# One fused transformer block on one core: gate tiles, table lookups, load order and the last norm rearranged

## The chip, the cores and the metric

One core of a Trainium2 chip. The metric is device microseconds (us) of one execution; the number for a kernel is the median of its runs. Engines: PE is TensorE (matmul), DVE is VectorE, ACT is ScalarE, POOL is GpSimd, SP is SyncE, which here only issues loads.

## The reference, cut to what matters

512 tokens of width 2048 pass three sublayers, each followed by `layer_norm(ALPHA * x + h)`:

```
h = hybrid_mixer(x)            # chunked mLSTM branch + 16-head forgetting attention,
                               # each branch times sigmoid(gate), summed, times w_out
h = memory_cross_attention(x)  # 4 heads on 256 memory rows
h = peer_ffn(x):
    q  = x @ w_pq;  sc = q . sub_keys                # 8 heads, 2 x 128 keys
    top_s, top_i = top_k(sc, 16)                     # per half
    best_s, best_pos = top_k(top_s0[:,None] + top_s1[None,:], 16)
    idx = (top_i0 * 128 + top_i1)[best_pos];  g = softmax(best_s)
    out = sum_k gelu(x . expert_u[idx_k]) * g_k * expert_v[idx_k]   # 128 of 16384 experts per token
```

All inputs and the output are float32.

## The kernel before, in words

**Matmuls.** A float32 product is made of three fp32r matmuls. `load_raw` (line 153) loads 1 MB of weights into a raw tile by the SP queue; `shares` (170) casts it to the high part with ACT (line 183, two casts of 1024 columns) and subtracts for the low part with DVE (188) into a ring tile; `group_ws` (198) and `group_as` (237) multiply. Where the next raw tile lies is given by `raws["pools"]`, a rotation over pools. All loads of weights are on the SP queue, which takes them in order; which order that is, is set by a scheduler that simulates the program and may place instructions of one engine otherwise than they were written, unless `after` (96) ties two of them.

**Tokens.** Tokens 0 to 127 pass first (`ml0`, `fx0`), then 128 to 511 as one block of 384 (`ml1` from 564, `fx1` from 649). In `ml1` sigmoid gates were stored to `sgd` in DRAM; for each of four groups lines 639 to 641 load four of them back into `qk` tiles (six buffers), ahead of that group's weights on the SP queue; line 645 stores the products to `mg`, by ACT's queue, out of the same tiles. In `fx1` the 16 attention heads run inside the pool `fxa`; the first of the four gate groups (`wi[28]`) is woven into heads 12 to 14, but its sigmoids (655) write into the pool `fxg`, which opens only when `fxa` has been closed.

**Experts, first 256 tokens.** `job_u` and `job_v` gather one expert row per token from DRAM by POOL's indirect DMA (1034) and use it with one DVE instruction of 2048 columns (1054, 1070). `tick` hands out these jobs: each ring share adds `rate * cost * mult` to a credit, and a full credit starts a job. 256 jobs for tokens 128 to 255 are handed out from 2910 us on, at `rate = 256 / 980`, with `mult` 0.65 in the selection stage, 1.5 in the building of the gates, 0.86 after it.

**Experts, last 256 tokens.** No gather here: every expert is multiplied.

- Selection (loop at 1365): `Choice.run` makes scores and `select` (926) picks 16 of 128 per half. Its positions are turned into indices by comparing with `iota`, multiplying with the indices and summing (964 to 966), once per half, in f32. Between the eight selections `next_a` (1323) multiplies 1 MB of the expert table `uT` each: three times, seven times at the last. The raw tiles lie in `wp`, in `rw`, opened on the right side of SBUF, and in `gap`.
- Building (1382 to 1414): the gate of each expert and token is the product of two one-hot matrices. For four tokens at a time DVE compares `i1` and `i0` with `iota` (1400, 1403, 128x512 f32), ACT scales the second in place (1406), PE multiplies (1407), ACT copies out (1412). Two calls of `next_a` stand at its start, then one for every second quad.
- Main loop (`stage_o`, 1456): 8 groups of 16 expert blocks, each for two halves `dh` of the output width, 8 loads of `vD` per half. `stage_h` (1441) makes the gated activation of two blocks: it multiplies (1448) the stored or kept gelu (`gb`, `ga`) by the gate `G` and splits it (150, 151). All eight calls of a group fall into its first half, `dh == 0`, but for the first, which is made in the half before. `ask_g` and `ask_a` load what they need.
- End: `fin` (1513) and `fin_gathered` (1095) make the last norm on DVE with `fin_head` (1078, its square root on ACT) and `fin_tail` (1082), then store.

Of the kernel before, what the change touches and what calls it, by code (L numbers as in the profile page):

```python
# [21 lines left out]
P = 128  # L22
# [4 lines left out]
H = 256  # L27
# [22 lines left out]
def build(tc, I, out):  # L50
    nc = tc.nc
    NC_ = PKEYS
    with ExitStack() as ctx:
# [72 lines left out]
        ioti = cp.tile([P, P], I32, tag="ioti", name="ioti")  # L126
        nc.gpsimd.iota(ioti, pattern=[[1, P]], base=0, channel_multiplier=0)
        nc.vector.tensor_copy(iota, ioti)
# [13 lines left out]
        ei = [cp.tile([P, P], I32, tag=f"ei{t}", name=f"ei{t}") for t in range(2)]  # L142
# [10 lines left out]
        def load_raw(src, n=2048):  # L153
# [7 lines left out]
            nc.sync.dma_start(raw[:, :n], src)  # L161
# [125 lines left out]
        sgd = dp.tile([16, P, 384], F32, tag="sgd", name="sgd")  # L287
        mlk = dp.tile([ML_H, P, 256], F32, tag="mlk", name="mlk")
# [275 lines left out]
        def ml1(mp, X, hpool, hT):  # L564
# [73 lines left out]
            for g in range(4):  # L638
                sg = [mt("qk", 6, n) for _ in range(4)]
                for q in range(4):  # L640
                    nc.sync.dma_start(sg[q], sgd[g * 4 + q])

                def ev_b(s, b, sg=sg, g=g):
                    nc.vector.tensor_mul(sg[s], sg[s], b)
                    nc.scalar.dma_start(mg[g * 4 + s], sg[s])

                yield from group_ws(I["w_br_ml"][g], hT, 3, ev_b)

        def fx1(X, ypool, yT, galloc, G):
            n = 384  # L650
            sgf, gate_pool = [], []

            def ev_g(s, b):
                t = gate_pool[0].tile([P, n], F32, tag="sg", bufs=16, name=nm("sg"))
                nc.scalar.activation(t, b, AF.Sigmoid)  # L655
                sgf.append(t)

            g0 = group_ws(wi[28], X, 3, ev_g)
            with pool("fxa", side="right") as fp:
                def ft(tag, bufs, n=512):  # L660
                    return fp.tile([P, n], F32, tag=tag, bufs=bufs, name=nm(tag))

# [43 lines left out]
                for qd in range(4):  # L706
# [916 lines left out]
```

## Time and profile before

| | us |
|---|---|
| runs of the kernel | 4589.1, 4597.87, 4593.03; median 4593.03 |
| the profiled execution | 4602.5 |
| its span, first to last instruction | 4600.8 |
| PE, DVE, ACT, POOL busy | 4467.5, 3743.1, 2231.7, 871.0 |

The profile is of one execution. [...] DMA share is the mean busy share of the 16 DMA engines of the core. A wait is put down to what came last.

### The profile page before, as it was taken

Reading aid. Unit: us, or ns where it says so; the run is one execution under the profiler, and the core shown is the slowest. Engines: PE = TensorE matmul, PEld = TensorE weight load, DVE = VectorE, ACT = ScalarE, POOL = GpSimd, SP = SyncE. Lnnn points to the kernel's source line nnn. Section 1 sums busy time; section 2 is a strip of 40 time slices with the busy share of each in tenths; the row PEclk is TensorE's granted clock in tenths of the full one; section 3 lists DMA queues with packets and bytes.
Section 4 is the critical chain, followed back from the end, with each engine's and each line's share of the span. In section 5 each row is a group of like instructions: output and inputs, shape, how many; then the busy total and the mean of one; then the engine's idle time right before and its main releaser. Section 6 shows DMA issues by size and latency. Waiting matters only on the chain.

```text
span 4600.8 us, 65219 instructions
## 1 busy us (share of the span) xinstructions
PE 4467.5 (97%) x25702; PEld 3993.3 (87%) x25702; DVE 3743.1 (81%) x4326; ACT 2231.7 (49%) x3029; POOL 871.0 (19%) x631
## 2 busy tenths in 40 slices
PE   8999999999999999999999999898999999999997
PEld 7888888889888899999799777798998778999996
DVE  7877667657798877887778678799988988988888
ACT  6766766645344422333322585544774334434433
POOL 1000000000132222232122000011222323333332
PEclk9999999999999999999999999899999999999998
DMA  8898889766798889888789766786989999999997
GB/s 295 321 334 327 323 316 342 259 235 213 281 339 331 333 310 346 340 339 311 266 331 346 296 244 231 270 311 250 372 346 419 398 382 403 379 384 396 372 357 292
DMA packets 244019, 1488.70 MB, mean 324 GB/s; under 512 B 26588, under 2 KB 52252, under 8 KB 75392
## 3 DMA queue, kind: packets, MB, share of 16 engines
q1 hardware_dynamic: 150384, 888.47, 51.7%
q0 software_dynamic: 81664, 561.95, 31.2%
q10 hardware_dynamic: 11664, 34.12, 1.9%
q8 instruction: 201, 3.29, 0.3%
q14 instruction: 106, 0.87, 0.1%
HBM read 1425.15 MB, written 59.29 MB: 323 GB/s over the span
## 4 chain that ended last, share of the span: by engine, by line
PE 65%; DVE 6%; issue 5%; DMA 3%; POOL 1%; ACT 1%; DVEq 0%; SPq 0%; ACTq 0%; POOLq 0%
PE mm L209 22%; PE mm L259 6%; PE mm L251 6%; PE mm L252 6%; PE mm L1491 4%; PE mm L1490 4%; PE mm L1487 4%; PE pa L1343 4%; PE pa L1336 3%; PE pa L1339 3%; DVE ring L188 2%; POOL rows L1034 1%; DMA raw<-in_vD 1%; DVE rows L1054 1%; PE sm L700 1%
## 5 line engine op out<-in xcount | busy, mean ns | idle before, releaser
L183 ACT CAST ring<-raw 128x1024 fp32r<-128x1024 f32 x1568 | 1600.1, 1050 | 1528.4 <-PE mm L209 464.1
L188 DVE TENSOR_TENSOR ring<-raw,ring 128x2048 fp32r<-128x2048 f32 (+1 forms) x926 | 1813.2, 1961 | 542.5 <-ACT ring L183 267.8
L1034 POOL DMA_INDIRECT rows<-in_peer_u,ei x256 | 368.6, 1440 | 1634.9 <-DVE rows L1054 791.3
L209 PE MATMUL mm<-Ah,ring 128*128 128x384 f32 x2560 | 669.6, 341 | 2.4 <-ACT sg L655 2.4
L1034 POOL DMA_INDIRECT rows<-in_peer_v,ei x256 | 435.5, 1701 | 978.8 <-DVE x2l L1070 698.3
L1054 DVE SCALAR_TENSOR_TENSOR rows<-rows,x2l 128x2048 f32<-128x2048 f32 x256 | 583.9, 2284 | 34.2 <-DMA rows<-in_peer_u,ei 34.0
L1070 DVE SCALAR_TENSOR_TENSOR x2l<-rows,dots,x2l 128x2048 f32<-128x2048 f32 x256 | 600.7, 2347 | 11.9 <-DMA rows<-in_peer_v,ei 11.2
L1336 PE MATMUL pa<-Xh,ring 128*128 128x256 f32 x2048 | 495.0, 283 | 2.7 <-ACT ring L183 2.7
L1339 PE MATMUL pa<-Xl,ring 128*128 128x256 f32 x2048 | 492.0, 281 | 0.0
L209 PEld LDWEIGHTS mm<-Ah,ring 128*128 128x128 f32 x2560 | 462.9, 189 | 8.0 <-ACT sg L655 2.6
L209 PE MATMUL mm<-Al,ring 128*128 128x384 f32 x1280 | 429.1, 339 | 0.0
L1491 PE MATMUL mm<-ring,hpl 128*128 128x512 f32 x1024 | 394.8, 398 | 9.5 <-DVE hpl L151 9.5
L1490 PE MATMUL mm<-ring,hph 128*128 128x512 f32 x1024 | 393.4, 396 | 8.3 <-ACT ring L183 5.5
L1336 PEld LDWEIGHTS pa<-Xh,ring 128*128 128x128 f32 x2048 | 386.7, 189 | 6.1 <-ACT ring L183 3.5
L1339 PEld LDWEIGHTS pa<-Xl,ring 128*128 128x128 f32 x2048 | 387.5, 189 | 2.4
L251 PE MATMUL mm<-ring,Zh 128*128 128x512 f32 x832 | 328.1, 394 | 2.7 <-ACT ring L183 2.7
L252 PE MATMUL mm<-ring,Zl 128*128 128x512 f32 x832 | 328.7, 395 | 0.0
L251 PE MATMUL mm<-ring,Ah 128*128 128x512 f32 x768 | 307.5, 401 | 1.1 <-ACT ring L183 1.1
L252 PE MATMUL mm<-ring,Al 128*128 128x512 f32 x768 | 304.3, 396 | 0.0
L209 PE MATMUL mm<-Bh,ring 128*128 128x384 f32 x1024 | 263.2, 339 | 8.1 <-ACT ring L183 7.5
L1343 PE MATMUL pa<-Xh,ring 128*128 128x256 f32 x2048 | 265.8, 282 | 3.1 <-DVE ring L188 3.1
L1487 PE MATMUL mm<-ring,hph 128*128 128x512 f32 x1024 | 257.6, 392 | 2.4 <-DVE ring L188 2.2
(393 smaller groups left out, 7081.0 us busy)
## 6 DMA issues: line engine op xcount, KB each, us to landing
raw<-in_w_in SPq DMA_DIRECT2D x256, 1024.0 KB
raw<-in_uT SPq DMA_DIRECT2D x128, 1024.0 KB
raw<-in_vD SPq DMA_DIRECT2D x128, 1024.0 KB
raw<-in_w_out SPq DMA_DIRECT2D x48, 1024.0 KB
raw<-in_peer_wq SPq DMA_DIRECT2D x48, 1024.0 KB
raw<-in_w_xkv SPq DMA_DIRECT2D x32, 1024.0 KB
raw<-in_w_br_ml SPq DMA_DIRECT2D x32, 1024.0 KB
raw<-in_w_br_fx SPq DMA_DIRECT2D x32, 1024.0 KB
```

The source lines that it names most:

```text
L183: x = nc.scalar.copy(hi[:, c:c + 1024], src[:, c:c + 1024])
L188: s = nc.vector.tensor_sub(lo, src, hi.bitcast(F32))
L209: i = nc.tensor.matmul(o, w, x, start=start and s % per == 0, stop=stop and s % per == per - 1)
L251: nc.tensor.matmul(banks[t], xh[:, tt], wh[:, c], start=k == 0, stop=False)
L252: nc.tensor.matmul(banks[t], xl[:, tt], wh[:, c], start=False, stop=False)
L1034: i = nc.gpsimd.indirect_dma_start(out=rows, out_offset=None, in_=I[table], in_offset=bass.IndirectOffsetOnAxis(ap=ei[t][:, k:k + 1], axis=0))
L1054: i = nc.vector.scalar_tensor_tensor(rows, rows, 1.0, tok[t]["x2l"], op0=ALU.mult, op1=ALU.mult, accum_out=d[:, k % GB:k % GB + 1])
L1070: i = nc.vector.scalar_tensor_tensor(acc, rows, d[:, GB + k % GB:GB + k % GB + 1], acc, op0=ALU.mult, op1=ALU.add)
L1336: i = nc.tensor.matmul(bank, uh[:, sl], xh, start=k == 0, stop=False)
L1339: nc.tensor.matmul(bank, uh[:, sl], xl, start=False, stop=False)
L1490: nc.tensor.matmul(banks[t][g], a[:, tt], vh[:, gs_], start=c == c0, stop=False)
L1491: nc.tensor.matmul(banks[t][g], b[:, tt], vh[:, gs_], start=False, stop=False)
```

## The change

It consists of eight edits, A to H.

- A: the gate weights are loaded by the SP queue in place of ACT's.
- B: in `ml1` the four `sgd` loads of a group come after the group's second load of weights.
- C: in `fx1` the first two gate groups write into tiles of `fxa` and are stored to a new DRAM tensor `fgd`; the first is woven into all of heads 12 to 15, the second follows inside `fxa`. Groups 2 and 3 stay; `fgd` is loaded during group 3.
- D: `rw` is opened on the left side, after `gap`; the rotation and its start change; the next six loads of weights are tied to their written order; `keysT` is loaded after the third load of a group.
- E: `select` looks up both halves together, in bf16: ACT copies the indices to bf16, repeated 16 times, and DVE makes one compare, one multiply and one sum of 1024 columns.
- F: nine calls of `next_a` at the last selection, and none at the start of the building; `mult` 0.7 in place of 0.65 in the selection.
- G: in the building `i0` is compared in bf16, four tokens innermost; ACT scales out of that tile, reading every fourth element, into a new f32 tile.
- H: `stage_h` is called in both halves, every second load; in the last norm the subtraction of the mean and the product with the weight come before the square root's chain, and the last additions to `acc` are tied behind the first product of the gathered tokens' norm.

```diff
 A            gw = gp.tile([P, 16, 68], F32, tag="graw", name="gw")
-            nc.scalar.dma_start(gw, I["gate_w"])
+            nc.sync.dma_start(gw, I["gate_w"])
 B (ml1)
-                sg = [mt("qk", 6, n) for _ in range(4)]
-                for q in range(4):
-                    nc.sync.dma_start(sg[q], sgd[g * 4 + q])
+                sg = []
...
-                yield from group_ws(I["w_br_ml"][g], hT, 3, ev_b)
+                for i, _ in enumerate(group_ws(I["w_br_ml"][g], hT, 3, ev_b)):
+                    yield
+                    if i == 1:
+                        for q in range(4):
+                            sg.append(mt("qk", 6, n))
+                            nc.sync.dma_start(sg[q], sgd[g * 4 + q])
 C (fx1)
+                def gate_out(g):
+                    def ev(s, b):
+                        t = ft("c", 10, n)
+                        nc.scalar.activation(t, b, AF.Sigmoid)
+                        nc.scalar.dma_start(fgd[4 * g + s], t)
+                    return group_ws(wi[28 + g], X, 3, ev)
...
+                    g0 = gate_out(0)
                     for s in range(4):
-                        if qd == 3 and s < 3:
+                        if qd == 3:
                             yield next(g0)
                         fox_head(4 * qd + s, ...)
+                yield from gate_out(1)
             with pool("fxg", side="right") as gp:
-                gate_pool.append(gp)
-                yield from g0
-                for g in range(1, 4):
-                    yield from group_ws(wi[28 + g], X, 3, ev_g)
+                sgf = [gp.tile([P, n], F32, tag="sg", bufs=16, name=nm("sg")) for _ in range(16)]
+                for g in (2, 3):
+                    for i, _ in enumerate(group_ws(wi[28 + g], X, 3, ev_g)):
+                        yield
+                        if g == 3:
+                            for q in (2 * i, 2 * i + 1):
+                                nc.sync.dma_start(sgf[q], fgd[q])
 D
-        rw = rws.enter_context(pool("rw", side="right"))     # before xs.close(), bb.close()
+        rw = rws.enter_context(pool("rw"))                   # after gap is opened
-        raws["pools"], raws["one"] = [wp, rw, wp, rw, gap], gap
+        raws["pools"], raws["one"], raws["n"] = [wp, rw, wp, gap, rw], gap, -1
+        raws["order"] = (6, None)
...
-                        yield from group_ws(I["peer_wq"][g], X2, 2, ev_q)
+                        for i, _ in enumerate(group_ws(I["peer_wq"][g], X2, 2, ev_q)):
+                            yield
+                            if i == 2:
+                                after(ld.dma_start(ks, I["keysT"][:, 4 * g:4 * g + 4]), raws["last"])
 E (select)
-                ixf = w("ixf", [4, 16])
-                nc.vector.tensor_copy(ixf, ix)
+                ids = w("ids", [4, 16, 16], BF16, bufs=1)
+                nc.scalar.copy(ids, ix.unsqueeze(3).to_broadcast([P, 4, 16, 16]))
...
-                for q, n in ((0, "i0"), (1, "i1")):
-                    eq = w("eq", [2, 16, 16], bufs=1)
-                    nc.vector.tensor_tensor(eq, pf[:, q]..., it, op=ALU.is_equal)
-                    nc.vector.tensor_mul(eq, eq, ii[:, :, q]...)
-                    nc.vector.tensor_reduce(out=sel[n][t][:, sl]..., in_=eq, axis=AX.X, op=ALU.add)
+                eq = w("eq", [4, 16, 16], BF16, bufs=1)
+                nc.vector.tensor_tensor(eq, pf..., ranks..., op=ALU.is_equal)
+                nc.vector.tensor_mul(eq, eq, ids)
+                nc.vector.tensor_reduce(out=self.ids[t][:, :, sl]...,
+                                        in_=eq.rearrange("p (q h) r k -> p q h k r", q=2), axis=AX.X, op=ALU.add)
 F
-        state["mult"] = 0.65
+        state["mult"] = 0.7
-                    for i in range(7 if steps == 8 else 3):
+                    for i in range(9 if steps == 8 else 3):
...
-            if t == 0:
-                next_a()
-                next_a()
 G
-                    o0 = gp.tile(full, F32, tag="o0", bufs=3, name=nm("o0"))
-                    nc.vector.tensor_tensor(o0, selT["i0"][:, ta:ta + 4].unsqueeze(2).to_broadcast(full), it,
+                    o0 = gp.tile([P, P, 4], BF16, tag="o0", bufs=2, name=nm("o0"))
+                    nc.vector.tensor_tensor(o0, selT["i0"][:, ta:ta + 4].unsqueeze(1).to_broadcast([P, P, 4]), keys4,
                                             op=ALU.is_equal)
+                    og = gp.tile(full, F32, tag="og", bufs=2, name=nm("og"))
-                        hold = nc.scalar.activation(o0[:, u], o0[:, u], AF.Copy, scale=...)
+                        hold = nc.scalar.activation(og[:, u], o0[:, :, u], AF.Copy, scale=...)
 H (stage_o, fin, fin_gathered)
-                    nxt = c0 + 2 * jj + 2 if dh == 0 else c0 + J
-                    if nxt < c0 + J or (dh and jj == 6 and not last):
-                        stage_h(nxt)
+                    due = c0 + J + 2 * (jj // 2 + 1) if dh else c0 + (2 * jj + 4 if c0 == 0 else J // 2 + jj + 2)
+                    while nxt_h[0] < min(due, NC_, c0 + J + J // 2):
+                        stage_h(nxt_h[0])
+                        nxt_h[0] += 2
...
-                if dh and not last and jj < 2:
-                    ask_g(c0 + J + 4 * jj)
-                    ask_a(c0 + J + 2 + 2 * jj)
...
-                        nc.vector.tensor_add(o, o, banks[t][g])
+                        i = nc.vector.tensor_add(o, o, banks[t][g])
+                        if last and dh:
+                            after(i, first_norm)
...
+            nc.vector.bn_aggr(st[:, 24:26], st[:, 0:24])
+            for q in range(2):
+                fin_low(acc..., st, lw[0]...)       # (a - mean) * w
             fin_head(st)                            # 1 / sqrt(var + eps)
             for q in range(2):
-                fin_tail(acc[:, sl], st, lw[0][:, sl], lw[1][:, sl])
+                fin_high(acc..., st, lw[1]...)      # a * rstd + b
```

## Rows read from the trace of the kernel before

**Rows 1.** The page: the line of its first part (busy us, share, instructions), the granted clock in 40 slices, and from its fifth part the group of the casts (busy us, mean ns | idle before).
```profile
PE 4467.5 (97%) x25702; PEld 3993.3 (87%) x25702; DVE 3743.1 (81%) x4326; ACT 2231.7 (49%) x3029; POOL 871.0 (19%) x631
...
PEclk9999999999999999999999999899999999999998
...
L183 ACT CAST ring<-raw 128x1024 fp32r<-128x1024 f32 x1568 | 1600.1, 1050 | 1528.4 <-PE mm L209 464.1
```

**Rows 2.** Busy time by stretch. Columns: stretch, its length, busy us of PE, PEld, DVE, ACT and POOL with the count of instructions, granted clock, DMA share, GB/s.
```profile
1674.00:1690.00 16.00, 8.53 (x34) 8.21 (x33) 6.34 (x5) 2.78 (x3) 1.88 (x2) 0.68 0.66 265
2266.00:2300.00 34.00, 25.85 (x112) 18.87 (x111) 15.58 (x44) 11.70 (x27) 2.08 (x2) 0.86 0.39 140
2906.00:2932.00 26.00, 12.98 (x93) 12.27 (x91) 12.05 (x15) 10.48 (x16) 2.19 (x2) 0.74 0.67 252
3060.00:3180.00 120.00, 120.00 (x1013) 120.00 (x1012) 116.02 (x262) 50.98 (x57) 20.19 (x16) 1.00 0.81 306
3180.00:3210.00 30.00, 14.80 (x95) 13.75 (x94) 28.81 (x103) 11.52 (x26) 0.00 (x0) 0.66 0.30 117
3210.00:3420.00 210.00, 202.77 (x1695) 200.29 (x1695) 193.70 (x210) 157.16 (x409) 50.85 (x31) 1.00 0.90 350
...
3584.00:3607.00 23.00, 19.43 (x74) 15.05 (x73) 19.00 (x20) 7.13 (x8) 4.84 (x3) 0.87 0.94 371
3674.00:3710.00 36.00, 32.42 (x128) 25.66 (x127) 30.99 (x28) 14.39 (x17) 7.27 (x6) 0.91 0.95 376
3787.00:3810.00 23.00, 19.43 (x77) 15.09 (x76) 23.00 (x21) 8.39 (x10) 6.19 (x4) 0.93 0.90 342
3900.00:4500.00 600.00, 597.83 (x3851) 545.41 (x3850) 522.75 (x295) 244.44 (x270) 205.01 (x103) 1.00 0.95 379
...
4574.00:4601.00 27.00, 0.89 (x4) 0.37 (x2) 22.89 (x45) 0.61 (x3) 0.00 (x0) 0.56 0.29 117
```

**Rows 3.** The DMA queues: one issue of the whole program, with its size.
```profile
gw<-in_gate_w ACTq DMA_DIRECT2D x1, 544.0 KB
```

**Rows 4.** The chain of work that ended last, 1640 to 1695 us: start, us, what (xcount).
```profile
1643.62 9.33 PE mm L209 x54
...
1653.84 12.52 DMA mg<-qk
...
1667.03 15.45 DMA raw<-in_w_br_ml
...
1683.68 11.43 PE mm L209 x49
```

**Rows 5.** The same chain, end of the attention heads, 2220 to 2300 us.
```profile
2294.45 1.28 ACT L655
2295.75 0.50 ACT sg L655
2296.29 3.86 PE mm L209 x13
```

**Rows 6.** What the SP queue issued, 2850 to 2920 us: start, us, line, what (xcount, merged).
```profile
2888.48 24.42 SPq L161 DMA_DIRECT2D raw<-in_uT  x3
2913.00 0.41 SPq L161 DMA_DIRECT2D raw<-in_peer_wq  x1
```

**Rows 7.** The chain of work that ended last, 2905 to 2945 us.
```profile
2912.55 0.14 DVE ei L1020
...
2913.00 10.37 DMA raw<-in_peer_wq
...
2924.49 13.44 PE mm L209 x96
```

**Rows 8.** DVE's instructions in the selection stage, 2930 to 3200 us, by line and shape: busy us, mean ns of one | idle before.
```profile
L188 DVE TENSOR_TENSOR ring<-raw,ring 128x2048 fp32r<-128x2048 f32 x42 | 95.7, 2278 | 4.8 <-PE mm L209 3.8 <-issue 0.9
L1054 DVE SCALAR_TENSOR_TENSOR rows<-rows,x2l 128x2048 f32<-128x2048 f32 x29 | 66.1, 2281 | 5.0 <-DMA rows<-in_peer_u,ei 5.0
L964 DVE TENSOR_TENSOR eq<-pf,iota 128x512 f32<-128x512 f32 x16 | 11.0, 685 | 0.0
L965 DVE TENSOR_TENSOR eq<-eq,ixf 128x512 f32<-128x512 f32 x16 | 10.9, 684 | 0.0
L966 DVE TENSOR_REDUCE sel_i<-eq 128x32 f32<-128x512 f32 x16 | 10.9, 681 | 0.0
...
L980 DVE TENSOR_TENSOR sel_g<-sel_g,s 128x256 f32<-128x256 f32 x1 | 0.4, 420 | 0.0
```

**Rows 9.** The building of the gates, 3206 to 3425 us: two groups by line.
```profile
L1406 ACT ACTIVATE o<-o,gT 128x128 f32<-128x128 f32 x241 | 75.9, 402 | 13.2 <-DVE o L1403 12.6 <-DVE o L1400 0.4
...
L1403 DVE TENSOR_TENSOR o<-i0T,iota 128x512 f32<-128x512 f32 x60 | 40.8, 683 | 0.0
```

**Rows 10.** Who PE waited for, 3440 to 3860 us: us in total, times, longest.
```profile
PE mm L1491 <- DVE hpl L151: 9.5, 3, 3.2
```

**Rows 11.** DVE in order of time, 3580 to 3612 us: start, us, line, what [idle before].
```profile
3591.08 2.48 DVE L1502 SCALAR_TENSOR_TENSOR acc<-acc,mm 128x512 f32<-128x512 f32 x4 [4.00 <-PE mm L1487]
```

**Rows 12.** DVE in order of time, 4500 to 4601 us.
```profile
4573.76 2.48 DVE L1504 TENSOR_TENSOR acc<-acc,mm 128x512 f32<-128x512 f32 x4 [5.22 <-PE mm L1487]
4576.15 2.46 DVE L1099 BATCH_NORM_STATS2 fst<-x2l 128x6 f32<-128x512 f32 x4
...
4581.32 2.48 DVE L1083 SCALAR_TENSOR_TENSOR x2l<-x2l,fst,lw 128x1024 f32<-128x1024 f32 x2
```

More of the change, by code (lines that the diff above doesn't have):

```diff
@@ L125, in build @@
         iota = cp.tile([P, P], F32, tag="iota", name="iota")
-        ioti = cp.tile([P, P], I32, tag="ioti", name="ioti")
-        nc.gpsimd.iota(ioti, pattern=[[1, P]], base=0, channel_multiplier=0)
-        nc.vector.tensor_copy(iota, ioti)
+        ei = [cp.tile([P, P], I32, tag=f"ei{t}", name=f"ei{t}") for t in range(2)]
+        nc.gpsimd.iota(ei[0], pattern=[[1, P]], base=0, channel_multiplier=0)
+        nc.vector.tensor_copy(iota, ei[0])
+        ranks = cp.tile([P, 16, 16], BF16, tag="ranks", name="ranks")
+        nc.vector.tensor_copy(ranks, iota[:, 0:16].unsqueeze(2).to_broadcast([P, 16, 16]))
         def const_in(name, shape):
@@ L160, in load_raw @@
                 raw = p.tile([P, 2048], F32, tag="raw", bufs=1 if p is raws.get("one") else 2, name=nm("raw"))
-            nc.sync.dma_start(raw[:, :n], src)
+            i = raws["last"] = nc.sync.dma_start(raw[:, :n], src)
+            if raws.get("order"):
+                if raws["order"][1] is not None:
+                    after(i, raws["order"][1])
+                raws["order"] = (raws["order"][0] - 1, i) if raws["order"][0] > 1 else None
             return raw
@@ L287, in build @@
         sgd = dp.tile([16, P, 384], F32, tag="sgd", name="sgd")
+        fgd = dp.tile([8, P, 384], F32, tag="fgd", name="fgd")
         mlk = dp.tile([ML_H, P, 256], F32, tag="mlk", name="mlk")
@@ L909, in __init__ @@
                 self.tp, self.nb, self.lean, self.gate = tp, nb, lean, None
-                self.sel = {n: [pl.tile([P, P], F32, tag=f"{n}{t}", name=nm(f"sel_{n}{t}")) for t in range(nb)]
-                            for n in ("i0", "i1")}
+                self.ids = [pl.tile([P, 2, P], F32, tag=f"i{t}", name=nm(f"sel_i{t}")) for t in range(nb)]
+                self.sel = {n: [i[:, q] for i in self.ids] for q, n in ((0, "i0"), (1, "i1"))}
                 self.gates = pl.tile([P, nb, P], F32, tag="g2", name=nm("sel_g"))
@@ L1380, in build @@
         gp = gs.enter_context(pool("gbuild", side="right"))
-        selT = {n: gp.tile([P, H], F32, tag=n + "T", name=n + "T") for n in ("i0", "i1", "g")}
+        selT = {n: gp.tile([P, H], d, tag=n + "T", name=n + "T") for n, d in (("i0", BF16), ("i1", F32), ("g", F32))}
+        keys4 = gp.tile([P, P, 4], BF16, tag="keys4", name="keys4")
+        nc.vector.tensor_copy(keys4, iota.unsqueeze(2).to_broadcast([P, P, 4]))
         for t in range(HB):
@@ L1401, in build @@
                                             op=ALU.is_equal)
[L1402 to L1403 removed]
+                    o0 = gp.tile([P, P, 4], BF16, tag="o0", bufs=2, name=nm("o0"))
+                    nc.vector.tensor_tensor(o0, selT["i0"][:, ta:ta + 4].unsqueeze(1).to_broadcast([P, P, 4]), keys4,
                                             op=ALU.is_equal)
+                    og = gp.tile(full, F32, tag="og", bufs=2, name=nm("og"))
                     for u in range(4):
[L1406 to L1407 removed]
+                        hold = nc.scalar.activation(og[:, u], o0[:, :, u], AF.Copy, scale=selT["g"][:, ta + u:ta + u + 1])
+                        nc.tensor.matmul(bank[:, u * P:(u + 1) * P], o1[:, u], og[:, u], start=True, stop=True)
                     if q % 2:
@@ L1514, in fin @@
             st = fst[t]
+            nc.vector.bn_aggr(st[:, 24:26], st[:, 0:24])
+            for q in range(2):
+                sl = slice(q * 1024, (q + 1) * 1024)
+                fin_low(acc[t][:, sl], st, lw[0][:, sl])
             fin_head(st)
```

53 lines of the change are left out of this document (24 added, 29 removed).

## The prediction, made before the change was run

> **What bounds the kernel now.** I read the page's busy line and its clock by slices first. PE has a matmul in flight for 4467.5 of 4600.8 us [rows 1], so the whole kernel is paced by PE, and what can be won without removing matmuls is the 133 us in which PE has none, plus the time in which the granted clock is below full after such a hole. The change removes no matmul, so only these holes count. The second view is the busy time by stretch: it shows that the holes are not spread evenly. From 3900 to 4500 us PE misses 2 us of 600; in six short stretches it misses 3 to 15 us each, and in these the granted clock is also down, 0.66 to 0.93 as a mean [rows 2]. The third view, the chain of waits, says for each hole what was late; the fourth, an engine in order of time, says why. The eight edits are priced hole by hole.
>
> **Edit B, the `sgd` loads.** PE is idle 7.5 of the 16 us at 1674, and the 49 matmuls behind the hole take 11.43 us where 54 took 9.33 before it, so they lose about 3 us to the lower clock [rows 2, 4]. The chain: the stores of the last products to `mg` (12.52 us) release the `qk` tiles, only then does SP issue the `sgd` loads, and behind them stands the next weight load, which lands 15.45 us later [rows 4]. With B two weight loads stand ahead of the wait, 96 matmuls at 0.173 us or 16.6 us of PE work, more than the 12.52 us store. Gain 10 us, ends 7 and 10.5. SP still waits there; what is late next is the third weight load.
>
> **Edit C, the gates behind the heads.** In 2266 to 2300 PE is idle 8.2 us, at a mean clock of 0.86, because the last heads have almost nothing beside them [rows 2]; then a table load (1.28 us) and a sigmoid stand before the first matmul, and 13 matmuls take 3.86 us, 1.6 more than at 0.173 [rows 5]. With C the rest of the first gate group and all of the second (96 x 2 matmuls, 33 us) need no new pool and can lie beside heads 14 and 15. New: 8 stores and 8 loads of 192 KB, 3.1 MB or some 9 us of DMA at the 350 GB/s of a busy stretch [rows 2], but spread over 70 us in which PE has no hole; the 8 loads stand on SP between weight loads into tiles long free, and two more table loads of 1.28 us fall on ACT, which works 11.7 of 34 us there. Those are covered; without the cover they would cost 2.6 us. Gain 9 us, ends 4 and 11.5.
>
> **Edit D, the start of the selection.** PE is idle 13.0 of the 26 us at 2906, and the 96 matmuls after it take 13.44 us where 96 at 0.118 take 11.4 [rows 2, 7]: 15 us in all. SP issued three `uT` loads from 2888 to 2913 ahead of the fourth `peer_wq` load, which PE needed first; it left SP at 2913.00, released by the indices of the block before (`ei`), and took 10.37 us to land [rows 6, 7]. With D the written order is kept, so this load goes first, and `rw` no longer lies where those indices keep tiles. I cannot see from the trace when the tiles beneath the new place come free; the norm of the block before runs until 2910, so the fifth load may wait that long, which PE would not feel, since four loads of 48 matmuls are 22.6 us. `keysT` now waits behind the third load on SP and can hold the fourth until the same tiles are free, which would leave some of the hole. Gain 11 us, ends 3 and 15.
>
> **Edit E, the lookup.** Per selection six instructions of 0.68 us go, 4.1 us of DVE [rows 8], and three of 1024 columns come. The trace has no two-operand DVE instruction in 16 bit. By elements, one costs 2278 / 2 = 1.14 us or a little more; by bytes, as 128x512 in f32, 0.68 us [rows 8]. [...] I take 0.9 for each of the other two, halfway, so E saves about 1.1 us of DVE per selection (0.6 to 1.5), 8 selections here, 9 us. ACT gains a copy of 1024 columns, 1.05 us [rows 1], and is half idle in this stage (50.98 of 120 us) [rows 2]. The trace shows a sum of 512 columns at 0.68 us over adjacent elements only [rows 8]. [...] No row here reads strided, so the bounds above stand.
>
> **Edits E and F, the end of the selection.** Here DVE is the limit: 116 of 120 us from 3060 to 3180 and 28.8 of 30 us after, while PE is idle 15.2 of the last 30 and then runs at a low clock, mean 0.66, some 3 us [rows 2]. F puts two calls of `next_a` (48 matmuls at 0.118, 5.7 us each, 11.4 us) from the building into this hole. They bring DVE two shares (4.6 us) and, with the ticks at the higher rate, about 1.5 + 2.4 jobs of 2.28 us, 9 us [rows 8], while E gives back 9. Half of the added jobs fall early in the stage, where DVE has slack, so DVE ends about 4 us later; the building loses 11.4 us of PE work. Gain 11.4 - 4, and 1 us of clock: 8 us, ends 3 and 14. Hidden behind this: the jobs moved here are missing from the building, and their number over the kernel is the same.
>
> **Edit G, the building.** PE is idle 7.2 of 210 us; DVE works 194, ACT 157, DMA is 0.90 busy [rows 2]. The 64 compares of 0.683 us [rows 9] become 0.42 each if bytes count (the 128x256 f32 row) or stay [rows 8]: 0 to 17 us of DVE. I take 0.55, 8 us, which lets DVE run ahead and closes part of PE's idle time: 2 us, ends -2 and 6, the lower one because the scaled tile now has two buffers where it had three. The trace shows f32 compares alone, at a time per element. [...]
>
> **Edit H, `stage_h` in both halves.** At the three stretches from 3584, 3674 and 3787 PE is idle 3.6 us each and runs at a mean clock of 0.87 to 0.93 [rows 2]; three waits for the low half `hpl` sum to 9.5 us [rows 10]. At the first, DVE waits 4.00 us for PE, makes four additions of `acc`, and only then the share and the activation that PE needs next [rows 11]. By count of matmuls: 74, 128 and 77 where 23, 36 and 23 us at 0.23 hold 100, 157 and 100, so 78 matmuls or 18 us are missing. With H four pairs of activations exist at each border. What is late next is the bank that the additions must free, about 0.7 us, and the weight share behind them. Gain 12 us, ends 5 and 16. From 3900 on 2 us are missing, and there is nothing to gain.
>
> **Edit H, the end.** The last matmul ends at 4574; then 27 us of DVE. Before it DVE is idle 5.22 us, although the gathered tokens' sums are complete: their statistics (2.46 us) and first product (2.48 us) come after the additions [rows 12]. The new tie puts these 4.9 us into the idle time. Gain 5 us, ends 2 and 6. **Edit A:** 544 KB off the first transfers are some 1.3 us at 416 GB/s and more [rows 2, 3]: 1 us, ends 0 and 1.5.
>
> **The sum.** 1 + 10 + 9 + 11 + 8 + 2 + 12 + 5 = 58 us; all lower ends give 22, all upper ends 81. The profiled execution took 4602.5 us, so 4544.5 by its own time; that execution lies 9.5 us above the median of the runs, 4593.03, and by the median the forecast is 4535 us.
>
> **Rivals.** (1) *The holes close, but DMA and DVE give a part back.* DMA is at 0.90 to 0.95 and DVE at 84 to 100% from 3060 us on [rows 2]; an earlier start there only meets the next wait. Then B, C and A hold (20 us), the end holds (5), and of D to H between a fifth and a third comes through, 10: 35 us, 4558. For it: those shares. Against: from 3900 to 4500 the same shares leave PE without a hole. (2) *A new wait on SP's queue takes the place of the one removed.* D and B only move loads that wait for tiles; if `keysT`, `sgd` or the fifth load holds a weight load as long as before, B and D give 0: 37 us, 4556. That both fail is unlikely, since the chain names what held each. (3) *Slower: ACT in the building.* Its scaling now reads every fourth element of a 16-bit tile. There are 256 of them at 0.402 us [rows 9], and ACT is busy 157 of 210 us [rows 2]. If a strided read cost 1 us, ACT would need 157 + 240 x 0.6 = 301 us, 91 more than the stretch lasts: with the other 56 us of gain that is 35 us slower, 4628. It decides from about 0.87 us each on (157 + 240 x 0.47 = 270, 60 over); below 0.62 it costs nothing. Nothing in the trace reads ACT's input so. (4) *The change does not do what it says,* as far as 16 bit goes: no compare is faster. Then E saves 5 in place of 9 and G gives 0: 6 us less, 4541, inside the forecast.
>
> **How the numbers follow.** A measurement of this kernel can tell about 0.2%, 9 us. Forecast with (4): 0.66; (1): 0.18; (2): 0.09; (3): 0.04; 0.03 for ends that cancel. The forecast's own range is 4512 to 4558. The range over the cases reaches from all upper ends, 81 us, less the spread of the runs, to the sum of all lower ends (4571), rounded: 4506 to 4570. Faster 0.92, same 0.04, slower 0.04.
>
> **What would show it right or wrong.** Right: in the profile after, no wait of `peer_wq` behind `uT`, the stretches that answer to 1674, 2266, 2906 and the three borders without a hole above 2 us and at a clock of 1.0, compares of 1024 columns between 0.61 and 1.2 us, and DVE busy in the 5 us before the last matmul. Wrong: ACT scalings above 0.5 us, PE idle at the end of the selection as long as before, or a new wait of SP for tiles in front of weights. A time above 4571 would mean that the holes moved instead of closing.

## The result and the profile after

The changed kernel took 4570.82 us (median of 4 runs, 4567.12 to 4573.15) beside 4595.45 of the kernel before on the same chip: ratio 0.9944, interval 0.9929 to 0.996. That is 25 us faster where 58 were forecast, just outside the range of 4506 to 4570. The profiled execution took 4572.07 us with a span of 4570.0, 30.8 under that of before. The lines of its page that answer to [rows 1]:

```profile
PE 4461.2 (98%) x25702; PEld 3983.3 (87%) x25702; DVE 3724.8 (82%) x4264; ACT 2252.1 (49%) x3051; POOL 900.4 (20%) x631
...
PEclk9999999999999999999999999999999999999999
...
L188 ACT CAST ring<-raw 128x1024 fp32r<-128x1024 f32 x1568 | 1597.1, 1050 | 1456.8 <-PE mm L214 454.1
```

The matmuls are the same 25702. The busy time by stretch, for the stretches of [rows 2] moved to where the same work now stands (columns as there), and one more, 3456 to 3578:

```profile
1665.00:1681.00 16.00, 14.77 (x85) 14.45 (x85) 10.65 (x10) 3.26 (x4) 4.30 (x3) 1.00 0.99 405
2244.00:2278.00 34.00, 34.00 (x199) 32.32 (x199) 29.18 (x38) 14.87 (x24) 5.82 (x6) 1.00 0.88 313
2881.00:2907.00 26.00, 20.86 (x145) 19.10 (x145) 15.74 (x28) 18.12 (x28) 3.68 (x2) 0.87 0.90 344
3155.00:3185.00 30.00, 13.31 (x86) 12.44 (x85) 28.94 (x88) 10.14 (x23) 0.94 (x1) 0.66 0.20 79
3185.00:3395.00 210.00, 203.94 (x1676) 200.67 (x1675) 178.57 (x204) 159.36 (x408) 36.99 (x31) 0.99 0.90 351
3456.00:3578.00 122.00, 112.98 (x528) 92.30 (x527) 103.03 (x91) 46.42 (x56) 32.13 (x19) 0.94 0.99 395
3567.00:3590.00 23.00, 22.69 (x97) 17.70 (x96) 22.33 (x20) 9.24 (x11) 7.03 (x4) 1.00 1.02 415
3656.00:3692.00 36.00, 35.65 (x153) 28.07 (x152) 33.22 (x30) 13.81 (x16) 9.97 (x6) 1.00 1.02 419
3763.00:3786.00 23.00, 22.38 (x95) 17.68 (x96) 23.00 (x21) 7.78 (x9) 7.28 (x4) 1.00 1.00 400
3875.00:4475.00 600.00, 598.46 (x3855) 546.02 (x3854) 523.98 (x295) 245.09 (x271) 215.03 (x103) 1.00 0.96 380
4548.00:4570.00 22.00, 0.88 (x4) 0.37 (x2) 18.30 (x37) 0.41 (x2) 0.00 (x0) 0.62 0.35 143
```

The holes of B, C and of the three borders are gone, and that at 2906 is mostly closed. The hole at the selection's end is as it was (PE 13.31 of 30 us, granted clock 0.66 of full). Worse than before is the stretch from 3456 to 3578: PE 113 of 122 us at a clock of 0.94, with DMA at 0.99. The same work in the kernel before:

```profile
3475.00:3592.00 117.00, 110.28 (x534) 91.23 (x533) 98.24 (x84) 46.38 (x54) 31.03 (x20) 0.97 1.01 412
```

So DMA was as busy there before, and PE missed 6.7 us in place of 9.0. In the changed kernel the chain of waits goes through transfers of 1 MB that take 21 us, 18 to 19 in that stretch before and 10.37 in [rows 7]. After:

```profile
3432.89 21.00 DMA rows<-in_peer_u,ei
...
3460.73 21.02 DMA raw<-in_vD
...
3519.97 21.25 DMA raw<-in_vD
```

Before:

```profile
3476.48 18.82 DMA raw<-in_vD
...
3533.44 18.00 DMA raw<-in_vD
```

To compare kernels I count the columns of the matmuls, which are the same in all, and read when PE has issued 3.2, 4.2, ... million of them (a "mark"). "Lost" is the time in a stretch without a matmul, plus the rest weighted by what the granted clock is below full. The three stretches are the selection's end with the building (6.49 to 6.88 million), the building's end with the first group of the main loop (to 7.27) and the three borders (to 7.82). From the traces, in us (one profiled execution of each kernel; "median" is that of all its runs):

```
kernel             at 3.2    4.2  6.02 M   lost: select  first  borders   at 7.82  9.2 M   span   median
before             1528.1 2013.8  2939.6          24.4   11.1     20.2     3860.8 4489.6  4600.8  4595.5
changed            1527.9 2004.8  2913.7          23.4   21.2      5.5     3835.6 4463.6  4570.0  4570.8
before_bc          1528.2 2005.4  2911.6          23.9   11.4     21.8     3836.7 4465.4  4576.7  4579.1
no_e               1525.2 2000.6  2910.7          29.5   14.9      7.8     3834.0 4462.5  4569.0  4572.7
no_f               1526.3 2007.6  2917.1          22.5   11.0      3.4     3823.7 4452.0  4560.3  4560.7
no_g               1526.7 2002.0  2908.2          25.0   17.9      4.3     3822.1 4454.6  4561.1  4568.3
no_h               1526.9 2002.3  2908.3          24.7   21.6     14.0     3840.1 4468.0  4574.4  4569.4
half_bytes         1527.2 2009.8  2917.5          22.8   20.9     10.9     3841.3 4469.6  4576.1  4570.8
no_h_half_bytes    1527.0 2006.5  2916.1          26.7   20.8     16.2     3849.8 4477.0  4583.4  4582.4
half_bytes_early   1525.5 2004.9  2911.9          22.5    3.6      6.5     3813.2 4444.6  4551.0  4554.7
mid_select         1523.9 2001.4  2910.0          18.7   17.1     11.8     3827.3 4455.8  4563.6  4570.1
mid_select_2       1525.7 2001.1  2908.0          19.9   18.8     11.0     3827.0 4454.4  4563.3  4571.7
shift              1528.8 2005.1  2915.0          23.8   15.6      1.8     3819.4 4448.2  4583.4  4585.7
no_h_shift         1531.4 2006.8  2912.7          23.0   16.0     17.1     3831.3 4460.2  4594.8  4596.6
no_f_shift         1528.2 2005.2  2913.0          23.3   12.7      2.2     3814.9 4443.8  4578.4  4580.8
mid_shift          1524.6 2004.4  2913.3          15.8   19.4      4.0     3818.4 4447.2  4571.5  4580.2
no_f_shift_2       1528.0 2007.8  2916.5          24.7   16.0      2.9     3825.6 4453.9  4587.5  4588.0
best               1525.1 2000.4  2906.5          17.4   15.3      2.6     3808.6 4436.8  4567.1  4576.0
no_f_halves        1527.2 2009.7  2919.4          17.6   21.2      7.0     3832.7 4459.5  4565.9  4555.4
no_f_halves_shift  1530.6 2009.9  2916.6          15.9   11.3      2.0     3811.9 4441.0  4555.5  4557.2
```

The 26 us that the change has won when the selection begins are still there at 7.82 million columns, 25; what the borders give (14.7) the first group has for the most part taken (10.1).

Behind the last mark the changed kernel takes 106.4 us, the kernel before 111.2. VectorE is idle 1.38 us ahead of its last additions, in place of the 5.22 of [rows 12]:

```profile
4547.74 2.48 DVE L1529 TENSOR_TENSOR acc<-acc,mm 128x512 f32<-128x512 f32 x4 [1.38 <-PE mm L1515]
```

### The profile page after: what moved, and what is told of

It reads as the page before. It is cut to its first block, busy times and chain, and to the rows that moved or that the text cites. A ratio compares the mean times of both kernels' runs of the same rounds, so it can differ in the third digit from the quotient of the medians.

```text
span 4570.0 us, 65174 instructions
## 1 busy us (share of the span) xinstructions
PE 4461.2 (98%) x25702; PEld 3983.3 (87%) x25702; DVE 3724.8 (82%) x4264; ACT 2252.1 (49%) x3051; POOL 900.4 (20%) x631
## 4 chain that ended last, share of the span: by engine, by line
PE 64%; DVE 6%; issue 5%; DMA 3%; ACT 1%; POOL 1%; DVEq 0%; ACTq 0%; POOLq 0%
PE mm L214 21%; PE mm L264 6%; PE mm L256 5%; PE mm L257 5%; PE mm L1519 4%; PE mm L1515 4%; PE mm L1518 4%; PE pa L1369 4%; PE pa L1362 3%; PE pa L1365 3%; DVE ring L193 2%; DMA raw<-in_vD 2%; DMA rows<-in_peer_u,ei 1%; DVE rows L1075 1%; PE sm L632 1%
## 5 line engine op out<-in xcount | busy, mean ns | idle before, releaser
L1055 POOL DMA_INDIRECT rows<-in_peer_u,ei x256 | 384.9, 1504 | 1607.8 <-DVE rows L1075 759.4
L1055 POOL DMA_INDIRECT rows<-in_peer_v,ei x256 | 448.8, 1753 | 947.8 <-DVE x2l L1091 642.8
L1518 PE MATMUL mm<-ring,hph 128*128 128x512 f32 x1024 | 403.6, 396 | 9.3 <-ACT ring L188 5.3
L1515 PE MATMUL mm<-ring,hph 128*128 128x512 f32 x1024 | 257.3, 392 | 4.7 <-DVE ring L193 4.6
```

The source lines that it names most:

```text
L1055: i = nc.gpsimd.indirect_dma_start(out=rows, out_offset=None, in_=I[table], in_offset=bass.IndirectOffsetOnAxis(ap=ei[t][:, k:k + 1], axis=0))
L1518: nc.tensor.matmul(banks[t][g], a[:, tt], vh[:, gs_], start=c == c0, stop=False)
```

## The experiments

**What the lead comes from: `before_bc`.** The kernel before with B and C of the diff and nothing else.

> The kernel before with B and C alone. By the changed kernel's profile at equal work they gain 9 and 13.5 us up to 2490 us. Theory 1, a lead taken ahead of 2900 us carries to the end, since the DMA-bound stretch starts with the selection and has its own length: 4571 to 4577 us. Theory 2, part of it is given back there: 4580 to 4590 us. By my forecast 19 us: 4574 us.

4579.14 us, ratio 0.9965 (0.9953 to 0.9977): 18 us, 2 us above theory 1's range and 1 us under theory 2's. Up to the selection it runs like the changed kernel, within 3 us at every mark. So A and D gave nothing that can be seen. D's hole closed without D; PE's wait in the kernel before, from 2880 to 2930, and in `before_bc`, from 2885 to 2911:

```profile
PE mm L209 <- ACT ring L183: 12.9, 1, 12.9
```

```profile
PE mm L209 <- ACT ring L183: 3.7, 1, 3.7
```

The fourth `peer_wq` load still goes behind two `uT` loads, but it leaves 20.5 us after the first of them, not 24.5 as before, and PE goes on 6.4 us later, not 11.5; these last 5 us lie in the transfer, which the chain of `before_bc` has at 5.32 us in place of 10.37:

```profile
2889.13 5.32 DMA raw<-in_peer_wq
```

Why, I did not test. It may be that the hole of 13 us belongs to the one profiled execution of the kernel before: that one took 4602.5 us, 6 to 9 above the medians, while `before_bc` is ahead of it by 28 us when the selection begins but by 18 in the medians.

**What takes the lead back: `half_bytes`, `half_bytes_early`.** Gathers that fetch half of the columns; VectorE works on the half twice. Part of the outputs is left out. The second run has the condition on gathers 60 to 89 of the second block:

```diff
+n = D // 2 if state.get("half") else D      # half: groups 1 to 4 of the main loop
+n = D // 2 if table == "peer_u" and t == 1 and 60 <= k < 90 else D      # half_bytes_early
-... indirect_dma_start(out=rows, in_=I[table], ...)
+... indirect_dma_start(out=rows[:, 0:n], in_=I[table].rearrange("n (q c) -> (n q) c", q=2) if n < D else I[table], ...)
```

> The changed kernel, but the gathers that the first four groups of the main loop issue (65 of 512) fetch 1024 of 2048 columns, VectorE working on the fetched half twice, so that its time stays; the outputs that come from the other halves are left out. It takes 34 MB, 83 us of DMA time at 410 GB/s, out of the stretch of 468 us. Theory 1, DMA sets that stretch: it falls to 442 to 452 us, total 4545 to 4556 us. Theory 2, waits on staging and buffers set it: total 4565 to 4573 us.

> The changed kernel, but 30 gathers of the second half (60 to 89, which run on the chip from about 3300 us to 3557 us) fetch half of their columns; the outputs that come from the other halves are left out. It takes 15.7 MB, 38 us of DMA time at 410 GB/s, out of the stretch that the earlier run with half bytes did not reach. Theory 1, the 21.3 us that TensorE loses from 3368 to 3578 us are DMA at its limit (share 1.0 from 3400 to 3560): they fall below 12 us, total 4556 to 4564 us. Theory 2, they come from the order in which the building ends, with the last rows of G stored late: 18 to 22 us stay, total 4568 to 4574 us.

The first gave 4570.80, ratio 0.9945 (0.9931 to 0.9958), the change's own time, and seemed to fell theory 1. But the first half-sized gather was issued only at some 3555 us, near 80 us after the main loop's first matmul, and behind the loss of the first group. With the early gathers halved: 4554.71, ratio 0.9914 (0.9901 to 0.9927), 16 us under the change. The building's end and the first group, in this run:

```profile
3365.00:3449.00 84.00, 81.48 (x672) 80.30 (x672) 66.98 (x90) 50.83 (x112) 20.07 (x13) 1.00 0.78 302
3449.00:3557.00 108.00, 106.89 (x531) 89.16 (x530) 103.80 (x126) 44.72 (x53) 42.72 (x20) 1.00 0.97 370
```

PE misses 1 of 108 us at a full clock, VectorE at 104: 3.6 us lost in place of 21.2. So DMA bytes bound this stretch. They do not bound the next, the borders: `half_bytes` has a DMA share of 0.82 to 0.92 there and no gain.

**H's borders: `no_h`, `no_h_half_bytes`, `no_h_shift`.** `stage_h` and its loads called as before:

```diff
-due = ...
-while nxt_h[0] < min(due, NC_, c0 + J + J // 2): ...
+nxt = c0 + 2 * jj + 2 if dh == 0 else c0 + J
+if nxt < c0 + J or (dh and jj == 6 and not last):
+    stage_h(nxt)
```

> The changed kernel with one part undone: the rows of H are staged again as before (all for the second half at its start, one pair at jj 6 of the first). Theory 1, the stretch of the first four groups of the main loop is set by its DMA bytes (share 1.0 there): the holes at the borders (about 19 us of lost TensorE time against 4) come back, but the elapsed time of that stretch at equal work stays within 5 us of the changed kernel's 468 us, total 4568 to 4577 us. Theory 2, the border holes add up to the time as I forecast: total 4583 to 4590 us.

> Both edits at once: H staged as before and the 65 gathers at half their bytes (the rest of their columns left out). Theory 1: with DMA out of the way the border holes cost what I forecast, 10 to 16 us more than with the half bytes alone, total 4557 to 4570 us. Theory 2: as with H undone alone, 4583 to 4590 us, so the half bytes give nothing.

> H's staging undone and the 16 gathers moved. With DMA bound, undoing H alone changed nothing. If that was because DMA took back what the borders gave, the borders count now: 8 to 14 us above the run with the shift alone, 4562 to 4574 us. If H's borders are worth nothing of themselves: within 3 us of it.

Undone alone: 4569.36, ratio 0.9947 (0.9934 to 0.9961), no difference from the change, although the borders lose 14.0 in place of 5.5. Undone with `half_bytes`: 4582.37, 11.6 us slower (0.9966, 0.9952 to 0.9979, against 0.9945); undone with `shift`: 4596.56, 10.9 us slower (1.0001, 0.9992 to 1.001, against 0.998, 0.997 to 0.9989). Both end above the times expected, but the differences are those of the first theories. So H's borders are worth 11 us, as forecast, where DMA has less to move. Why the plain pair does not show it stays open. Its runs lie from 4568.9 to 4576.3, so a few us can hide there, and in the profiled executions `no_h` loses no more in the first group (21.6 against 21.2) but is 5.4 us ahead when the selection begins.

**F: `no_f`, `mid_select`, `mid_select_2`.** F undone; or three calls more, inside the last `select` (one after its second, one after its fourth `top16`, one after those of the candidates). `mid_select_2` has eight calls ahead, these three, and one at the building's start.

```diff
-for i in range(9 if steps == 8 else 3):
+for i in range(7 if steps == 8 else 3):      # no_f, and at the start of the building:
+    if t == 0:
+        next_a(); next_a()
...
+    if j % 2:                                # mid_select, in select
+        self.mid()                           # next_a, in the last selection
```

> The changed kernel with F undone: seven calls of next_a at the last selection and two at the start of the building, as before (the multiplier stays 0.7). In the order made for it TensorE has 480 matmuls of next_a behind the building's last group, 400 in the changed kernel, 496 in the kernel before. Theory 1, F puts work ahead of the hole, not into it, and takes it from the building's start: undoing it leaves the hole at the selection's end at 15 to 17 us of idle and gives back up to 10 us of the 21.3 lost behind the building, since G is stored earlier; total 4560 to 4568 us. Theory 2, F is neutral: 4568 to 4574 us. As I forecast, F was worth about 7 us: 4575 to 4580 us.

> The changed kernel with three more next_a calls, issued inside the last selection of the topk stage (after its second and fourth top16 and after that of the candidates), three fewer between the building and the main loop. Theory 1, the 16.7 us hole at the end of the selection is 20 us of VectorE work with no share between: three shares in it put 16 us of matmuls into the hole for 6 us of VectorE, a gain of 5 to 11 us, total 4560 to 4566 us. Theory 2, what is gained there is given back in the DMA-bound stretch: total 4568 to 4573 us.

> As the run with calls of next_a inside the last selection, with eight calls ahead of it, three inside and one at the start of the building, where that run still idled 5.6 us. If the hole is work that is missing on TensorE while VectorE selects, the loss from the selection's end into the building falls from 23.4 us to 10 to 14 us, total 4558 to 4566 us. If what is gained there is lost again behind the building (17 to 21 us lost), 4567 to 4572 us.

`no_f`: 4560.70, ratio 0.9924 (0.991 to 0.9937), 10 us faster than with F, though the intervals just overlap (the change's begins at 0.9929). The hole is the same, the first group loses 11.0 in place of 21.2. What ends the hole in the changed kernel, PE's waits from 3155 to 3185:

```profile
PE mm L1415 <- DVE sel_i L983: 9.2, 1, 9.2
PE mm L1434 <- ACT og L1433: 5.6, 1, 5.6
```

VectorE's last share starts at 3154.6, and then it selects until 3177; before, 3175.1 and 3199.5. F's calls stand ahead of this tail, so the hole keeps its length. Calls inside the tail take 3.5 to 4.7 us off selection and building, and the medians show nothing (4570.10, ratio 0.9946, 0.9932 to 0.9959, and 4571.66, 0.9955, 0.9943 to 0.9968). In the profiled executions the borders lose 5 to 6 us more and the first group 2 to 4 less, and the span is 6 to 7 us shorter; but these lie 5 to 6 us under the runs' medians, so what takes the gain back is not shown.

**G and E: `no_g`, `no_e`.** G's compare back in 32 bits, three buffers, scaled in place; E's look-up in two halves of 32 bits, as in the code before.

> The changed kernel with G undone: i0 compared in 32 bits into three buffers and scaled in place by ScalarE. The compares take 0.68 us each instead of 0.42, 15 us more of VectorE over the building. In its order 640 matmuls of next_a stand behind the building's last group, 400 in the changed kernel. Theory 1, VectorE is not the building's bound and the two buffers and the later end of the building cost: 4560 to 4567 us. Theory 2, the 15 us of VectorE count: 4576 to 4586 us. As I forecast, G is worth 2 us: 4570 to 4575 us.

> The changed kernel with E undone: the two look-ups of a selection one after the other in 32 bits, compare and product 0.68 us and a sum of 512 columns each (0.6 to 1.2 us). By the rows of the changed kernel E saves some 0.5 to 0.7 us of VectorE per selection, and only the last one lies on the path: 4570 to 4574 us. As I forecast, E is worth more than 3 us: 4574 to 4580 us. If the sum over non-adjacent columns costs more than both sums did: 4566 to 4569 us.

`no_g`: 4568.32, ratio 0.9945 (0.9932 to 0.9959), between theory 1 and the forecast. The compare of 512 columns, in the changed kernel and here:

```profile
L1429 DVE TENSOR_TENSOR o<-i0T,keys 128x512 bf16<-128x512 bf16 x64 | 26.0, 423 | 8.6 <-ACT og L1433 8.5
```

```profile
L1427 DVE TENSOR_TENSOR o<-i0T,iota 128x512 f32<-128x512 f32 x64 | 43.4, 683 | 0.0
```

17 us of VectorE less are worth nothing that the runs show: the building does not wait for VectorE. The scaling out of the 16-bit tile on ACT:

```profile
L1433 ACT ACTIVATE og<-o,gT 128x128 f32<-128x128 bf16 x251 | 83.8, 420 | 1.7 <-DVE o L1429 1.7
```

`no_e`: 4572.67, ratio 0.9955 (0.9939 to 0.997): E gives 2 us, inside the spread, 6 by the lost time of select. Its rows in the changed kernel:

```profile
L983 DVE TENSOR_REDUCE sel_i<-eq 128x64 f32<-128x1024 bf16 x8 | 17.1, 2133 | 0.0
L980 DVE TENSOR_TENSOR eq<-pf,ranks 128x1024 bf16<-128x1024 bf16 x8 | 5.6, 696 | 0.0
L982 DVE TENSOR_TENSOR eq<-eq,ids 128x1024 bf16<-128x1024 bf16 x8 | 5.6, 694 | 0.0
```

3.52 us per selection where [rows 8] has 4.1: the sum takes back what compare and product save.

**Fewer bytes ahead, and a better sum.** `shift` moves 16 gathers behind the fourth group. `no_f_shift`, `no_h_shift` and `mid_shift` add one edit each. `no_f_shift_2` moves 10 (1.2, 1.06) with F undone, and `best` has the sum by halves besides:

```diff
-state["mult"] = 1.5
+state["mult"] = 1.0
+if c0 == 64:
+    state["mult"] = 1.02
...
-nc.vector.tensor_reduce(out=..., in_=eq.rearrange("p (q h) r k -> p q h k r", q=2), axis=AX.X, op=ALU.add)
+for n in (8, 4, 2):
+    nc.vector.tensor_add(eq[:, :, 0:n], eq[:, :, 0:n], eq[:, :, n:2 * n])
+nc.vector.tensor_add(..., eh[:, :, :, 0], eh[:, :, :, 1])
```

> The changed kernel with 16 gathers moved from the building (multiplier 1.5 becomes 1.0) to behind the first four groups of the main loop (0.86 becomes 1.02 from the fifth): 16.8 MB, 41 us of DMA time, leave the stretch from 3196 to 3836 us and go to where DMA idles some 60 us. Theory 1, that stretch is bound by DMA bytes and by the time in which DMA idles ahead of it: of the 26.7 us lost from 3368 to 3836 us under 13 stay, total 4553 to 4561 us. Theory 2, the load only moves: what is gained is lost behind 3860 us, total 4566 to 4575 us.

> F undone (which alone gave about 4561 us) and the same 16 gathers moved. If F costs by leaving DMA idle ahead of a stretch that DMA bounds, the two gains are largely the same one: within 4 us of the run with the shift alone, 4551 to 4560 us. If F costs something else, the gains add: 4542 to 4549 us.

> Three more calls of next_a inside the last selection and the 16 gathers moved. The calls alone gave 5 us by the profile up to the building and nothing by the medians. If DMA took that back, it stays now: 4 to 8 us under the run with the shift alone, 4546 to 4556 us. If the calls give nothing because VectorE's work is only moved: within 3 us of it.

> F undone and 10 gathers, not 16, moved from the building (multiplier 1.2) to behind the fourth group (1.06, so that the last gather is asked for a tenth of those groups' ticks earlier than with 1.02). If the DMA-bound stretch is the cause: the gain of F undone (4561 us) grows by 3 to 8 us and the wait of 27.7 us at the end is gone, 4552 to 4559 us. If moved gathers only come back as a late end: 4565 to 4580 us.

> The same with the sum of the selection's look-up made by four additions of halves in 16 bits in place of one strided sum over 1024 columns: 1.0 to 1.2 us per selection instead of 2.0 to 2.2. Where TensorE is never idle that is hidden; at the selection's end it shortens the hole by about 1 us. 0 to 2 us under the run beside it.

The first four, and `no_h_shift` above, end 20 to 36 us over their first ranges. `shift` (0.998) is 15.4 us ahead of the changed kernel at 9.2 million columns, much as theory 1 had it, though the first group and the borders still lose 17.4, not under 13; then it loses 29. Beside it the differences are as expected: `no_f_shift` (4580.78, 0.9968, 0.9956 to 0.998) is 5 us faster, so half of F's 10 is the same gain, and `mid_shift` (4580.18, 0.9964, 0.9951 to 0.9978) 5.5. In `no_f_shift_2` (4587.96), PE's waits from 4454 us on, and the chain there:

```profile
PE mm L1521 <- ACT ring L188: 29.8, 1, 29.8
```

```profile
4461.80 13.19 DMA rows<-in_peer_v,ei
...
4485.81 9.01 DMA rows<-in_peer_v,ei
...
4494.91 2.36 DVE x2l L1091
...
4497.29 8.39 DMA raw<-in_vD
```

A raw load waits for a gather's product: once all gathers are asked for, `load_raw` takes every second tile from the gathers' row buffers, and here gathers are still under way. So it is this kernel's rule that costs these 30 us. `best` (4575.97) is 12 us under `no_f_shift_2` (0.9959, 0.9946 to 0.9972, against 0.9982, 0.9973 to 0.9991), not 0 to 2. The four additions that replace the sum:

```profile
L984 DVE TENSOR_TENSOR eq<-eq 128x512 bf16<-128x512 bf16 x8 | 3.3, 418 | 0.0
L984 DVE TENSOR_TENSOR eq<-eq 128x256 bf16<-128x256 bf16 x8 | 2.3, 283 | 0.0
L986 DVE TENSOR_TENSOR sel_i<-eq 128x64 f32<-128x64 bf16 x8 | 1.8, 221 | 0.0
L984 DVE TENSOR_TENSOR eq<-eq 128x128 bf16<-128x128 bf16 x8 | 1.8, 220 | 0.0
```

1.14 us in place of 2.13, and three such sums lie in the select tail: PE's waits there fall from 16.8 to 10.6 us. That is 6 of the 12; in the profiles `best` is besides 10 us ahead when the selection begins, 7 of them up to 4.2 million columns, a mark at which the profiles differ by as much whatever the edit.

**The version that beats both: `no_f_halves`, `no_f_halves_shift`.** F undone and the sum by halves; then 16 gathers moved too (1.0, 1.06), and the row buffers kept from raw loads at the end:

```diff
-if raws["idle"] > 6 and raws["n"] % 2:
+if raws["idle"] > 6 and raws["n"] % 2 and len(jobs) <= 2 * NC_:
```

> F undone (alone 4561 us) and the sum by halves. By the profile of the last run against the one without it, the halves gain about 3 us in each of the two earlier selections and 6 us in the hole behind the last. Theory 1, DMA bounds the stretch from the selection on and takes the 6 us back: 4553 to 4557 us. Theory 2, all of it counts: 4545 to 4552 us. If the sum is hidden: 4559 to 4563 us.

> The same with 16 gathers moved from the building (1.0) to behind the fourth group (1.06), and raw loads kept out of the gathers' row buffers at the end (there, loads waited for the last gathers: 27 us of TensorE). Theory 1: the stretch loses 6 to 10 us less and nothing comes back at the end, 4540 to 4549 us, below the run beside it. Theory 2, late gathers cost at the end whatever buffers the loads take: 4560 us or more.

4555.37, ratio 0.991 (0.9894 to 0.9925), and 4557.23, ratio 0.9917 (0.9903 to 0.993): both beat the kernel before by 38 to 40 us and the change by some 15 (its interval begins at 0.9929, so the second's just touches it), and the shift adds nothing. The halves by themselves are worth 5 us (4555.37 against 4560.70 of `no_f`), inside the intervals, and `no_f_halves` is no earlier than `no_f` when the selection begins. In `no_f_halves_shift` the wait of 28 to 30 us is gone and PE is at 4441.0 at the last mark, but the last gathered rows arrive at 4525.5, when PE is all but done, and the end behind the last mark takes 114.5 us in place of 106.4. So both theories hold in part: the bytes leave the first groups, and come due at the end.

## Why the prediction was off

The direction was right, the size was not: 25 us in place of 58. By the runs: B 8, C 11, the end 5, H 11, E 2, F -10, A, D and G 0, together 27. That the sum comes near the measured 25 proves little: B, C and the end are read from single executions, E, F and H from medians, and H's 11 from pairs in which DMA has less to move; by the plain pair H gives 0 and the sum is 16.

- **B and C** (10 and 9) were right: `before_bc` gains 8.4 us up to 4.2 million columns, and 11.5 from there to 5.94 million (2852.9 us against 2872.8), and 18 in the medians. B's share is not sharp: from 3.2 to 4.2 million columns the kernels of the table that have B are 3 to 10 us faster than the kernel before, some of them under its lower end of 7.
- **The end** (5) was right: 106.4 us behind the last mark in place of 111.2. A (1) is not to be seen.
- **D** (11) failed: the same stretch without D, in `before_bc`, is as short. I read a chain in one execution and took the order of the loads for its cause. With the order unchanged, PE waited 3.7 us in place of 12.9: the load left SP 4 us sooner after the first `uT` load and took half as long to land. What made both longer in the profile of before stays open.
- **E and F** (8) failed at the step "F puts two calls of `next_a` from the building into this hole". They ran ahead of it; the hole is VectorE's tail behind its last share (22 us long, 24 before), and moving shares ahead of the tail leaves it: PE waits 16.7 us there, 15.2 before. Undone, F gives 10 us, and the profiles have them in the first group, for which the sum had no term. No run shows the 1.2 us at which E's sum was sized: the sum of 1024 columns took 2.13 in the changed kernel, one of 512 in 32 bits 0.68 before. Compare and product were sized at 0.9 and took 0.69, where the prediction's end "by bytes" had 0.68; so E saves 0.6 us per selection in place of 1.1.
- **G** (2): the compare took 0.42 us in place of 0.68, but this is hidden; 0 within the spread. The rival of a slow strided read on ACT fell: 420 ns in place of the 402 of [rows 9].
- **H's borders** (12) were right in size, 11 us in two pairs, but in the sum they met a loss that had no term: 10 us in the first group, where DMA bytes set the pace. By the profiles these are the same 10 us that F undone gives back. Rival 1 came nearest: it said that a lead is given back to DMA from 3060 us on, though it left 35 us. I gave it 0.18, since from 3900 to 4500 the same DMA share leaves no hole. That was the wrong stretch to judge by: there DMA runs at 0.96 and 380 GB/s, while in the first group it stands at 0.99 and 395 (1.01 and 412 before), a stretch for which [rows 2] has no row. But the share alone decides nothing: the borders run at 1.00 to 1.02 and 400 to 419 GB/s and lose only 5.5 us. Only taking bytes out told the two apart.
- **Two readings** of the prediction were loose, and neither moves the sum: [rows 2] has seven short stretches with holes, not six, and the 416 GB/s in A's term stand in no row shown (in the trace of before DMA moved that from 3539 to 3562 us).

Open: what makes the loss of the first group 11 us in some executions and 21 in others, with the same bytes in the whole program. F is not all of it, since `no_f_halves` shows 21.2 in its profile, which was the slowest of its runs (4567.6; the others 4549.2 to 4557.5). The scheduler orders the building anew for each edit: 400 matmuls of `next_a` stand behind its last group in the changed kernel, 480 in `no_f`, 432 in `no_f_halves`, 640 in `no_g`, 336 in `half_bytes_early`, and the loss does not simply follow that count.

## What to carry over

A hole closes only if work lands inside it: ask which engine's tail makes the hole and whether the moved work stands behind that tail's start in its queue. When leads are summed, check each stretch behind them for a second resource at its limit, by taking bytes out of exactly that stretch; where a request runs long after it is issued, look up which requests really fall into it. A stall read from one execution may be gone in the next program without its cure (PE's wait of 12.9 us was 3.7 in `before_bc`, without D); run the other edits without the one that is meant to cure it.

## What the runs showed of the hardware

A sum over 16-bit elements that lie 16 apart took 2.08 ns a column (1024 in 2.13 us, the changed kernel), against 1.33 for adjacent 32-bit ones (512 in 0.68 us, before), and four additions by halves did the same work in 1.14 us (`best`). ScalarE took 420 ns for 128 columns of a 16-bit tile with a step of four elements, against 402 for adjacent 32-bit ones. With weights and gathers together DMA moved 395 to 419 GB/s at a share of 0.99 to 1.02, and single transfers of 1 MB on the chain of waits took 21 us in the changed kernel's first group, against 10.4 (before) and 5.3 (`before_bc`) ahead of the selection.
